# Hybrid encoder kernel: every third expert-input weight tile is split by two DMAs, with slots of its own

## The chip, the cores and the metric

The kernel runs on one core of one Trainium2 chip. The metric is device time in microseconds (us), from one launch that computes both layers. The engines are named as in the profile: PE is TensorE's matmul, PEld its weight load, DVE is VectorE, ACT is ScalarE, POOL is GpSimd, SP is SyncE, which here only issues DMAs.

## The reference

Two layers over 256 tokens of width 1024, all in float32. A layer is a mixer (RMSNorm, one input projection, five groups of heads, a norm per group, one output projection, residual) and then a PEER expert layer. The expert layer is where the changed tiles are:

```python
q = (xn @ wq).reshape(b, s, PEER_HEADS, 2, PEER_HALF)
sc = jnp.einsum('bshjc,hjkc->bshjk', q, subkeys)
top_s, top_i = lax.top_k(sc, PEER_TOPK)
...
idx = i1 * PEER_N_KEYS + i2
g = jax.nn.softmax(best, axis=-1)
...
act = jax.nn.gelu(jnp.einsum('ckd,cd->ck', u_tab[ic], xc), approximate=False)
return jnp.einsum('ck,ckd->cd', (gc * act).astype(v_tab.dtype), v_tab[ic])
```

Each token takes 16 experts of 16384 in each of 8 heads. The kernel computes the products of every expert with every token and multiplies by a gate that is zero for experts that a token did not choose.

## The kernel before, in words

**Tiles.** All weights pass through one stream of 612 tiles of 128 x 1024 float32 (512 KB), 306 a layer: 4 of w_kv, 20 of w_in, 10 of w_out, 16 of wq, 128 of the expert table u_t, 128 of v_t. PE multiplies in the format fp32r. To keep float32's accuracy, each tile is split into a high part (w_hi, the tile cast to fp32r) and a low part (w_lo, the tile less its high part), and each product is three matmuls: w_hi with the high and with the low part of the other operand, and w_lo with its high part.

**Stream.** Class Stream (L56) does this. SP loads a tile into a raw slot (w_raw, L70; pool raw, three slots). ACT casts it into a high slot (w_hi, L82), DVE subtracts into a low slot (w_lo, L84; pool hl, three slots of each); in a few mixer tiles POOL subtracts. A raw slot is free when the subtraction has read it; high and low slots are free when PE's last matmul of that tile is done. `next` hands out the parts of the next tile, and `fill` runs the loads up to 4 and the splits up to 3 tiles ahead of the tile handed out. The splits are given high priority.

**Stages of a layer.** The mixer (L308) works on w_kv, w_in and w_out. Then the expert layer (`peer_phase`): 16 tiles of wq give queries; the U stage takes the tiles of u_t in pairs (`u_pair`, 24 matmuls of 256 columns a tile, L240 to L242) and puts the gelu of the products into a large tile H; the V stage takes the tiles of v_t (`v_units`, 12 matmuls of 512 columns a tile, L269 to L273). For V, H is split in its turn, two tiles at a time, into a_hi (ACT, L954) and a_lo (DVE, L956). Beside wq and the first U tiles the routing runs on DVE and POOL: scores, searches for the largest (L810 to L814), sums of candidates on POOL (L825, L828). Beside later U tiles the gates are made: DVE writes one-hot tiles (L901, L906), and PE multiplies them (L916, 16 matmuls for a pair of U tiles).

**What sets the order.** The program is written in the order above; a scheduler that goes by a model of the engines' times then fixes a queue for each engine, in which instructions run in order. A tile of a pool waits until the last reader of the slot's former tile is done.

Of the kernel before, what the change touches and what calls it, by code (L numbers as in the profile page):

```python
# [10 lines left out]
F32 = mybir.dt.float32  # L11
F32R = mybir.dt.float32r
# [4 lines left out]
ALU = mybir.AluOpType  # L17
# [3 lines left out]
P = 128  # L21
T = 256
D = 1024
NC = D // P
NK = 128
# [3 lines left out]
SPLIT_AHEAD = 300  # L29
LIMIT = 3  # L30
AFTER = 3
MEM_CHUNK = 2
# [23 lines left out]
class Stream:  # L56


    def __init__(self, tc, raw_pool, hl_pool, sources, ahead, split_ahead):
        self.tc, self.nc, self.raw_pool, self.hl_pool, self.sources = tc, tc.nc, raw_pool, hl_pool, sources  # L60
        self.ahead, self.split_ahead = ahead, split_ahead
        self.raw, self.parts = {}, {}
        self.n_raw = self.n_parts = self.pos = 0
        self.limit = len(sources)
        self.after = ()

    def fill(self, upto=None):
        while self.n_raw < min(len(self.sources), self.pos + self.ahead, upto or len(self.sources)):
            t = self.raw_pool.tile([P, D], F32, name="w_raw")
            self.last_load = self.nc.sync.dma_start(t, self.sources[self.n_raw][0])  # L70
            self.raw[self.n_raw] = t
            self.n_raw += 1
        while self.n_parts < min(self.n_raw, self.pos + self.split_ahead, self.limit):
            r = self.raw.pop(self.n_parts)
            with ExitStack() as ctx:
                ctx.enter_context(self.tc.high_priority(SPLIT_AHEAD))
                for ins in self.after:
                    ctx.enter_context(self.tc.issue_after(ins.ins))
                self.after = ()
                hi = self.hl_pool.tile([P, D], F32R, name="w_hi")  # L80
                lo = self.hl_pool.tile([P, D], F32R, name="w_lo")
                self.nc.scalar.copy(hi, r)  # L82
                on_pool = self.sources[self.n_parts][1]
                (self.nc.gpsimd if on_pool else self.nc.vector).tensor_sub(lo, r, hi.bitcast(F32))  # L84
            self.parts[self.n_parts] = (hi, lo)
            self.n_parts += 1

# [49 lines left out]
def build(tc, x, mem, w_in, w_kv, w_out, wq, u_t, v_t, subk, pool_w, conv_pw, vec, dist, inv_count, ind, out, depth=2,  # L137
          dbg=None):
    nc = tc.nc
    V, A, G = nc.vector, nc.scalar, nc.gpsimd  # L140

    sources = []

    def queue(aps, pool_every=0):
        sources.extend((ap, pool_every > 0 and n % pool_every == pool_every - 1) for n, ap in enumerate(aps))

    for l in range(depth):
# [3 lines left out]
        queue([wq[l, b] for b in range(16)])  # L151
        queue([u_t[l, i] for i in range(NK)])
        queue([v_t[l, i] for i in range(NK)])

    with (
        tc.tile_pool(name="const", bufs=1) as cp,
        tc.tile_pool(name="raw", bufs=3) as raw_pool,
        tc.tile_pool(name="hl", bufs=3) as hl_pool,
        tc.tile_pool(name="xn", bufs=1) as xp,
# [13 lines left out]

        ind_t = cp.tile([P, 3, P], F32, name="ind_t")
        ones_m, ind64, ind32 = ind_t[:, 0, :], ind_t[:, 1, :], ind_t[:, 2, :]
        iota_b = cp.tile([P, 16, 16], BF16, name="iota_b")
# [131 lines left out]
        def mixer_phase(l, mp, pa):  # L308
# [9 lines left out]
            def mt(shape, name, bufs=1, dt=F32, tag=None):  # L318
                return mp.tile(shape, dt, name=name, tag=tag or name, bufs=bufs)

            if not l:
                mem_t = mt([P, NC, T], "mem_t", tag="df_kz")
                mem_load(mem_t, vecs, FIRST)
                stream.fill()
                nc.sync.dma_start(ind_t, ind)
                nc.sync.dma_start(xt, x.rearrange("(a p) d -> p a d", p=P))
# [759 lines left out]
```

## Time and profile before

| what | us |
|---|---|
| median of 3 runs | 2009.11 (2007.75 to 2009.66) |
| the profiled execution, its own time | 2009.29 |
| its span, first to last instruction | 2007.1 |
| PE busy | 1965.0 (98%) |
| DVE busy | 1440.1 (72%) |
| ACT busy | 1005.3 (50%) |
| POOL busy | 153.0 (8%) |
| DMA: 331.5 MB, share of 16 engines on SP's queue | 48% |

Busy shares are averages over stages that differ. Mean durations of matmuls overlap, since PE is pipelined; what a matmul costs is read from the distance between starts, or from a stretch's length divided by its matmuls. PE's granted clock is 0.995 of full speed over the span.

### The profile page before, as it was taken

The numbers are of one execution on the slowest core, as the hardware profiler recorded it, in microseconds if no ns is written. First come the engines' busy times: TensorE is split into PE (matmuls) and PEld (weight loads), VectorE is DVE, ScalarE is ACT, GpSimd is POOL, SyncE is SP. The second block draws the span as 40 slices with busy tenths as digits, with TensorE's granted clock in tenths as the row PEclk, the third lists the DMA queues.
The fourth block names the chain that finished last, engine by engine and source line by source line (L and its number), as shares of the span: only waits on it lengthen the run. The fifth ranks groups of instructions, "written<-read, shape, count | busy, mean of one in ns | idle before, by whom it ended". The sixth has DMA issues, their size and how long they took to land.

```text
span 2007.1 us, 33754 instructions
## 1 busy us (share of the span) xinstructions
PE 1965.0 (98%) x13122; PEld 1808.6 (90%) x13122; DVE 1440.1 (72%) x2791; ACT 1005.3 (50%) x1482; POOL 153.0 (8%) x197
## 2 busy tenths in 40 slices
PE   8889999999999999999999999999999999999999
PEld 7878999999999888888898789999999998888887
DVE  6975899788985655555578668997889755555555
ACT  6664455444444544444476654644443444444443
POOL 3720000000000000000037200000000000000000
PEclk9999999999999999999999999999999999999999
DMA  6324455433445555555543244454434455555554
GB/s 215 116 74 163 170 175 171 162 137 137 147 148 183 200 195 189 190 193 193 189 165 116 84 168 168 169 179 148 148 134 140 149 187 189 190 195 192 189 191 155
DMA packets 92769, 331.50 MB, mean 165 GB/s; under 512 B 10817, under 2 KB 11713, under 8 KB 92353
## 3 DMA queue, kind: packets, MB, share of 16 engines
q1 hardware_dynamic: 92608, 329.34, 48.0%
q8 instruction: 103, 1.69, 0.3%
q14 instruction: 58, 0.47, 0.1%
HBM read 328.25 MB, written 1.05 MB: 164 GB/s over the span
## 4 chain that ended last, share of the span: by engine, by line
PE 89%; DVE 4%; POOL 2%; ACT 2%; issue 1%; DMA 0%; SPq 0%; DVEq 0%; POOLq 0%; ACTq 0%
PE ps_mm L240 15%; PE ps_mm L241 15%; PE ps_mm L242 15%; PE acc_v L270 12%; PE acc_v L273 12%; PE acc_v L269 12%; PE ps_g L916 6%; POOL cv_ac L438 1%; DVE w_lo L84 1%; PE ps_sc L804 1%; ACT w_hi L82 1%; PE acc_o L269 1%; PE acc_o L273 1%; PE acc_o L270 1%; PE ps_t L227 0%
## 5 line engine op out<-in xcount | busy, mean ns | idle before, releaser
L84 DVE TENSOR_TENSOR w_lo<-w_raw,w_hi 128x1024 fp32r<-128x1024 f32 x602 | 743.4, 1235 | 417.9 <-ACT w_hi L82 417.6
L82 ACT CAST w_hi<-w_raw 128x1024 fp32r<-128x1024 f32 x612 | 641.5, 1049 | 741.7 <-PE ps_mm L241 488.0
L240 PE MATMUL ps_mm<-xh,w_hi 128*128 128x256 f32 x2624 | 752.4, 288 | 0.3 <-ACT xh L230 0.3
L242 PE MATMUL ps_mm<-xh,w_lo 128*128 128x256 f32 x2624 | 745.7, 285 | 2.1 <-DVE w_lo L84 2.0
L241 PE MATMUL ps_mm<-xl,w_hi 128*128 128x256 f32 x2624 | 746.6, 285 | 0.0
L242 PEld LDWEIGHTS ps_mm<-xh,w_lo 128*128 128x128 f32 x2624 | 504.8, 192 | 3.6 <-DVE w_lo L84 2.9
L241 PEld LDWEIGHTS ps_mm<-xl,w_hi 128*128 128x128 f32 x2624 | 505.5, 193 | 0.9 <-DVE xl L231 0.5
L240 PEld LDWEIGHTS ps_mm<-xh,w_hi 128*128 128x128 f32 x2624 | 504.2, 193 | 1.4 <-ACT xh L230 0.9
L270 PE MATMUL acc_v<-w_lo,a_hi 128*128 128x512 f32 x1016 | 316.3, 392 | 0.0
L273 PE MATMUL acc_v<-w_hi,a_lo 128*128 128x512 f32 x1016 | 315.2, 392 | 0.0
L269 PE MATMUL acc_v<-w_hi,a_hi 128*128 128x512 f32 x1016 | 273.9, 391 | 0.0
L273 PEld LDWEIGHTS acc_v<-w_hi,a_lo 128*128 128x128 f32 x1016 | 190.8, 188 | 42.4
L269 PEld LDWEIGHTS acc_v<-w_hi,a_hi 128*128 128x128 f32 x1016 | 190.8, 188 | 41.9
L270 PEld LDWEIGHTS acc_v<-w_lo,a_hi 128*128 128x128 f32 x1016 | 190.9, 188 | 40.7
L954 ACT CAST a_hi<-H 128x512 fp32r<-128x512 f32 x128 | 79.4, 622 | 153.7 <-PE acc_v L270 150.1
L956 DVE TENSOR_TENSOR a_lo<-H,a_hi 128x512 fp32r<-128x512 f32 x128 | 88.6, 693 | 77.9 <-ACT a_hi L954 77.9
L906 DVE TENSOR_SCALAR ag<-iota_f,i1T,gT 128x128 f32<-128x128 f32 x512 | 142.4, 340 | 0.0
L916 PE MATMUL ps_g<-ag,a 128*128 128x128 f32 x1024 | 125.1, 275 | 0.0
L916 PEld LDWEIGHTS ps_g<-ag,a 128*128 128x128 f32 x1024 | 120.2, 192 | 0.0
L901 DVE TENSOR_TENSOR a<-iota_f,i2T 128x1024 f32<-128x1024 f32 x64 | 77.7, 1217 | 1.7 <-PE ps_g L916 1.7
L921 DVE TENSOR_TENSOR H<-ps_g,H 128x184 f32<-128x184 f32 (+31 forms) x128 | 58.8, 463 | 1.2 <-ACT H L920 1.2
L200 POOL MEMSET mm_kz<- 128x1024 f32 x2 | 1.9, 952 | 707.4 <-PE acc_v L260 707.4
(245 smaller groups left out, 1420.6 us busy)
## 6 DMA issues: line engine op xcount, KB each, us to landing
w_raw<-u_t SPq DMA_DIRECT2D x256, 512.0 KB, 3.3
w_raw<-v_t SPq DMA_DIRECT2D x256, 512.0 KB, 4.3
w_raw<-w_in SPq DMA_DIRECT2D x40, 512.0 KB, 3.3
w_raw<-wq SPq DMA_DIRECT2D x32, 512.0 KB, 3.3
w_raw<-w_out SPq DMA_DIRECT2D x20, 512.0 KB, 3.3
w_raw<-w_kv SPq DMA_DIRECT2D x8, 512.0 KB, 4.3
H<-subk SPq DMA_DIRECT2D x2, 1024.0 KB, 4.7
mem_t<-mem SPq DMA_DIRECT2D x4, 256.0 KB, 6.3
```

The costliest lines, as they stand in the source:

```text
L82: self.nc.scalar.copy(hi, r)
L84: (self.nc.gpsimd if on_pool else self.nc.vector).tensor_sub(lo, r, hi.bitcast(F32))
L240: nc.tensor.matmul(ps, wh, xh[:, c, :], start=(c == 0), stop=False)
L241: nc.tensor.matmul(ps, wh, xl[:, c, :], start=False, stop=False)
L242: nc.tensor.matmul(ps, wl, xh[:, c, :], start=False, stop=(c == NC - 1))
L269: nc.tensor.matmul(accs[tt][hf], ah[:, s], hi[:, n], start=start, stop=False)
L270: nc.tensor.matmul(accs[tt][hf], ah[:, s], lo[:, n], start=False, stop=False)
L273: nc.tensor.matmul(accs[tt][hf], al[:, s], hi[:, n], start=False, stop=False)
L906: V.tensor_scalar(ag[:, t, :], iota_f, i1T[:, k:k + 1], gT[:, k:k + 1], op0=ALU.is_equal, op1=ALU.mult)
L916: nc.tensor.matmul(ps[:, t, :], a2[:, 4 * q + t, :], ag[:, 4 * q + t, :], start=True, stop=True)
L954: A.copy(ah, src)
L956: V.tensor_sub(al, src, ah.bitcast(F32))
```

## The change

The list of sources now says how each tile is split: on DVE (an empty mark), on POOL, or by DMAs ("dma"). The last are the u_t tiles 9, 12, 15 and so on to 117, 37 in each layer: those whose number in the stream is 2 modulo 3, within tiles 8 to 119 of u_t. Such a tile is not loaded raw. POOL issues a DMA that casts it from DRAM into the high slot. ACT writes minus the high part into the low slot. POOL then issues a second DMA of the same float32 tile that adds to the low slot. The cast is put out up to 6 tiles ahead, the second step up to 5.

High and low slots come in two classes: tiles with a number of 2 modulo 3 (all of them, in every stage) have two slots of their own; the other two thirds share two. So there are four high and four low slots where there were three. Raw slots go from three to two, for all stages. A small table of indicators (ind_t) moves from a pool that lasts for the whole kernel into the mixer's pool, and is loaded in each layer.

```diff
+DMA_U = (8, 120)
+CAST_AHEAD = 6
+LOW_AHEAD = 5
...
+    def slots(self, n):
+        tag, self.last_slot = ("d", n) if n % 3 == 2 else ("", self.last_slot)
+        return [self.hl_pool.tile([P, D], F32R, name=name, tag=name + tag) for name in ("w_hi", "w_lo")]
...
+            src, how = self.sources[self.n_raw]
+            if how != "dma":
+                t = self.raw_pool.tile([P, D], F32, name="w_raw")
+                self.last_load = self.nc.sync.dma_start(t, src)
+                self.raw[self.n_raw] = t
             self.n_raw += 1
...
+            if self.sources[n][1] == "dma":
+                continue
...
-                hi = self.hl_pool.tile([P, D], F32R, name="w_hi")
-                lo = self.hl_pool.tile([P, D], F32R, name="w_lo")
+                hi, lo = self.slots(n)
                 self.nc.scalar.copy(hi, r)
...
+        while self.n_cast < min(end, self.pos + CAST_AHEAD):
+            src, how = self.sources[self.n_cast]
+            if how == "dma":
+                if self.last_slot < self.n_cast - 3:
+                    break
+                hi, lo = self.slots(self.n_cast)
+                self.nc.gpsimd.dma_start(hi, src)
+                self.parts[self.n_cast] = (hi, lo)
+            self.n_cast += 1
+        while self.n_low < min(self.n_cast, self.pos + LOW_AHEAD):
+            src, how = self.sources[self.n_low]
+            if how == "dma":
+                hi, lo = self.parts[self.n_low]
+                with self.tc.high_priority(SPLIT_AHEAD):
+                    self.nc.scalar.mul(lo, hi.bitcast(F32), -1.0)
+                    self.nc.gpsimd.dma_start(lo, src, accum_op=ALU.add)
+            self.n_low += 1
...
-        queue([u_t[l, i] for i in range(NK)])
+        for i in range(NK):
+            sources.append((u_t[l, i], "dma" if len(sources) % 3 == 2 and DMA_U[0] <= i < DMA_U[1] else ""))
...
-        tc.tile_pool(name="raw", bufs=3) as raw_pool,
-        tc.tile_pool(name="hl", bufs=3) as hl_pool,
+        tc.tile_pool(name="raw", bufs=2) as raw_pool,
+        tc.tile_pool(name="hl", bufs=2) as hl_pool,
...
+            ind_t = mt([P, 3, P], "ind_t")
+            ones_m, ind64, ind32 = ind_t[:, 0, :], ind_t[:, 1, :], ind_t[:, 2, :]
...
-                nc.sync.dma_start(ind_t, ind)
+            nc.sync.dma_start(ind_t, ind)
```

What the change does to the queues is shown at two places. In the rows below, the words in brackets are what an instruction waits for: DMAHW is a DMA that SP issued, DMASW one that POOL issued, the others are engines.

ACT's queue in the middle of the first V stage, before (the number behind a name tells one tile of it from the next):

```order
L954 CAST a_hi_8459<-H_1895 128x512 [waits PE_49]
L82 CAST w_hi_8425<-w_raw_8401 128x1024 [waits DMAHW4_49,DVE_49,PE_49]
L82 CAST w_hi_8443<-w_raw_8423 128x1024 [waits DMAHW5_49,DVE_49,PE_49]
L954 CAST a_hi_8499<-H_1895 128x512 [waits PE_49]
L82 CAST w_hi_8465<-w_raw_8441 128x1024 [waits DMAHW6_49,DVE_49,PE_49]
L82 CAST w_hi_8483<-w_raw_8463 128x1024 [waits DMAHW7_49,DVE_49,PE_49]
```

The same place in the changed kernel:

```order
L987 CAST a_hi_8422<-H_1895 128x512 [waits DVE_49,PE_49]
L97 CAST w_hi_8388<-w_raw_8364 128x1024 [waits DMAHW7_49,DVE_49,PE_49]
L97 CAST w_hi_8406<-w_raw_8386 128x1024 [waits DMAHW0_49,DVE_49,PE_49]
L987 CAST a_hi_8462<-H_1895 128x512 [waits PE_49]
L97 CAST w_hi_8428<-w_raw_8404 128x1024 [waits DMAHW1_49]
L97 CAST w_hi_8446<-w_raw_8426 128x1024 [waits DMAHW2_49,DVE_49,PE_49]
```

The sequence is the same; every third cast, that of a tile with slots of its own, has lost its wait for PE and waits for its load alone. SP's queue in V is a row of loads in both kernels, each waiting for a subtraction on DVE: of the tile whose raw slot it takes.

POOL's queue from the routing of the first half of the tokens (sums of candidates in H) onwards, before:

```order
L825 TENSOR_TENSOR H<-H 128x8x2 x3
L828 TENSOR_TENSOR H<-H 128x8x8 [waits DVE_49]
L825 TENSOR_TENSOR H<-H 128x8x16 [waits DVE_49]
L825 TENSOR_TENSOR H<-H 128x8x8 [waits DVE_49]
L825 TENSOR_TENSOR H<-H 128x8x5
```

The same place in the changed kernel:

```order
L858 TENSOR_TENSOR H<-H 128x8x2 x3
L861 TENSOR_TENSOR H<-H 128x8x8 [waits DVE_49]
L107 DMA w_hi<-u_t 128x1024 [waits PE_49,Activation_49]
L858 TENSOR_TENSOR H<-H 128x8x16 [waits DVE_49]
L116 DMA w_lo<-u_t 128x1024 [waits PE_49,Activation_49]
L107 DMA w_hi<-u_t 128x1024 [waits DVE_49,PE_49]
L116 DMA w_lo<-u_t 128x1024 [waits PE_49,Activation_49]
L107 DMA w_hi<-u_t 128x1024 [waits DMASW0_49,PE_49]
```

The DMAs of the split tiles now stand among the sums, in the same queue. Five tiles' DMAs (u_t 9 to 21) stand before the sums of the second half of the tokens, and the cast DMA of tile 24 stands behind most of them.

## Rows read from the trace of the kernel before

**Rows 1.** The page: busy time and share, and the chain that ended last, by engine.
```profile
PE 1965.0 (98%) x13122; PEld 1808.6 (90%) x13122; DVE 1440.1 (72%) x2791; ACT 1005.3 (50%) x1482; POOL 153.0 (8%) x197
...
PE 89%; DVE 4%; POOL 2%; ACT 2%; issue 1%; DMA 0%; SPq 0%; DVEq 0%; POOLq 0%; ACTq 0%
```

**Rows 2.** Stretches: mixer, three of U, V. Length, busy by engine, clock, DMA share, GB/s.
```profile
20.00:156.00 136.00, 122.55 (x854) 111.78 (x854) 103.50 (x180) 89.32 (x175) 63.87 (x55) 1.00 0.34 115
...
228.00:312.00 84.00, 84.00 (x705) 84.00 (x705) 80.06 (x329) 46.76 (x52) 6.22 (x18) 1.00 0.48 167
...
380.00:600.00 220.00, 220.00 (x1869) 220.00 (x1869) 189.51 (x391) 94.21 (x177) 0.00 (x0) 1.00 0.41 142
600.00:645.00 45.00, 45.00 (x377) 45.00 (x376) 24.42 (x24) 20.19 (x24) 0.00 (x0) 1.00 0.56 188
645.00:1010.00 365.00, 365.00 (x1650) 301.89 (x1649) 211.51 (x209) 177.19 (x207) 1.23 (x2) 1.00 0.57 192
```

**Rows 3.** Chain in order of time, U with gates: start, length, what (two successive pairs).
```profile
388.37 1.78 PE ps_g L916 x16
395.91 1.78 PE ps_g L916 x16
```

**Rows 4.** Timeline, V: start, length, engine, instruction, idle before and its releaser; SP merged.
```profile
700.61 0.62 ACT L954 CAST a_hi<-H 128x512 fp32r<-128x512 f32 x1 [1.23 <-PE acc_v L270]
...
701.14 1.05 ACT L82 CAST w_hi<-w_raw 128x1024 fp32r<-128x1024 f32 x1
...
702.22 1.23 DVE L84 TENSOR_TENSOR w_lo<-w_raw,w_hi 128x1024 fp32r<-128x1024 f32 x1 [0.26 <-ACT w_hi L82]
...
703.82 1.05 ACT L82 CAST w_hi<-w_raw 128x1024 fp32r<-128x1024 f32 x1 [1.63 <-PE acc_v L273]
...
704.90 1.23 DVE L84 TENSOR_TENSOR w_lo<-w_raw,w_hi 128x1024 fp32r<-128x1024 f32 x1 [1.46 <-ACT w_hi L82]
...
706.10 0.62 ACT L954 CAST a_hi<-H 128x512 fp32r<-128x512 f32 x1 [1.23 <-PE acc_v L270]
...
689.68 38.78 SPq L70 DMA_DIRECT2D w_raw<-v_t  x15
```

**Rows 5.** Raw loads, issue to landing: in 690 to 816, 380 to 590, 860 to 1000.
```profile
DMA to landing us min/median/max: 3.0/3.2/4.3
...
DMA to landing us min/median/max: 3.0/3.3/4.5
...
DMA to landing us min/median/max: 4.1/4.3/4.5
```

**Rows 6.** The start: one piece of the chain (DMA), then ACT, DVE and SP timelines.
```profile
2.12 6.03 DMA w_raw<-w_kv
...
8.17 1.04 ACT L82 CAST w_hi<-w_raw 128x1024 fp32r<-128x1024 f32 x1 [0.71 <-DMA w_raw<-w_kv]
...
6.68 1.23 DVE L84 TENSOR_TENSOR w_lo<-w_raw,w_hi 128x1024 fp32r<-128x1024 f32 x1 [2.55 <-ACT w_hi L82]
...
9.25 1.23 DVE L84 TENSOR_TENSOR w_lo<-w_raw,w_hi 128x1024 fp32r<-128x1024 f32 x1 [0.55 <-ACT w_hi L82]
...
4.46 0.46 SPq L70 DMA_DIRECT2D w_raw<-w_kv  x1
...
10.50 0.33 SPq L70 DMA_DIRECT2D w_raw<-w_in  x1
```

**Rows 7.** POOL's timeline: the sums for the second half of the tokens.
```profile
297.75 2.49 POOL L825 TENSOR_TENSOR H<-H 128x64 f32<-128x64 f32 x7 [57.52 <-DVE H L810]
...
300.93 0.42 POOL L825 TENSOR_TENSOR H<-H 128x128 f32<-128x128 f32 x1 [0.42 <-DVE H L813]
```

**Rows 8.** Raw loads issued in the first 9 us: issue to landing.
```profile
DMA to landing us min/median/max: 4.4/6.5/8.0
```

**Rows 9.** Line L906, the gates' one-hots: duration in ns (min/median/max), first and last start.
```profile
L906 DVE TENSOR_SCALAR ag<-iota_f,i1T,gT x512: 328/341/349, 314.3 to 1577.3; 128x128 f32<-128x128 f32 x171
```

More of the change, by code (lines that the diff above doesn't have):

```diff
@@ L62, in __init__ @@
         self.raw, self.parts = {}, {}
-        self.n_raw = self.n_parts = self.pos = 0
+        self.n_raw = self.n_parts = self.n_cast = self.n_low = self.pos = 0
+        self.last_slot = -1
         self.limit = len(sources)
         self.after = ()
+    def slots(self, n):
+        tag, self.last_slot = ("d", n) if n % 3 == 2 else ("", self.last_slot)
+        return [self.hl_pool.tile([P, D], F32R, name=name, tag=name + tag) for name in ("w_hi", "w_lo")]
     def fill(self, upto=None):
[L68 to L71, printed above, removed]
+        end = len(self.sources)
+        while self.n_raw < min(end, self.pos + self.ahead, upto or end):
+            src, how = self.sources[self.n_raw]
[3 more added lines that the diff above has]
+                self.raw[self.n_raw] = t
             self.n_raw += 1
         while self.n_parts < min(self.n_raw, self.pos + self.split_ahead, self.limit):
-            r = self.raw.pop(self.n_parts)
+            n = self.n_parts
+            self.n_parts += 1
+            if self.sources[n][1] == "dma":
+                continue
+            r = self.raw.pop(n)
             with ExitStack() as ctx:
@@ L79, in fill @@
                 self.after = ()
-                hi = self.hl_pool.tile([P, D], F32R, name="w_hi")
-                lo = self.hl_pool.tile([P, D], F32R, name="w_lo")
+                hi, lo = self.slots(n)
                 self.nc.scalar.copy(hi, r)
-                on_pool = self.sources[self.n_parts][1]
+                on_pool = self.sources[n][1] == "pool"
                 (self.nc.gpsimd if on_pool else self.nc.vector).tensor_sub(lo, r, hi.bitcast(F32))
-            self.parts[self.n_parts] = (hi, lo)
-            self.n_parts += 1
+            self.parts[n] = (hi, lo)
+        while self.n_cast < min(end, self.pos + CAST_AHEAD):
[15 more added lines that the diff above has]
+            self.n_low += 1
     def release(self, after):
@@ L144, in queue @@
     def queue(aps, pool_every=0):
-        sources.extend((ap, pool_every > 0 and n % pool_every == pool_every - 1) for n, ap in enumerate(aps))
+        sources.extend((ap, "pool" if pool_every > 0 and n % pool_every == pool_every - 1 else "") for n, ap in enumerate(aps))
     for l in range(depth):
@@ L172, in load_vecs @@
             return t
-        ind_t = cp.tile([P, 3, P], F32, name="ind_t")
-        ones_m, ind64, ind32 = ind_t[:, 0, :], ind_t[:, 1, :], ind_t[:, 2, :]
         iota_b = cp.tile([P, 16, 16], BF16, name="iota_b")
@@ L324, in mixer_phase @@
                 stream.fill()
-                nc.sync.dma_start(ind_t, ind)
+            nc.sync.dma_start(ind_t, ind)
+            if not l:
                 nc.sync.dma_start(xt, x.rearrange("(a p) d -> p a d", p=P))
```

## The prediction

> **What bounds the kernel now.** I read the page's busy shares and its chain first: TensorE (PE) is busy 98% of the span and is 89% of the chain that ended last [rows 1]. Then the busy time by stretch [rows 2]: from 228 to 1010 us, which is the whole U stage and V stage of a layer, PE is busy for the full length of every stretch. Its idle time, 42.1 us of 2007.1, lies in the mixers (13.5 us of the 136 in layer 0) and around the start and the ends. So in U and V the time is a number of matmuls times their step, and the reader should see that nothing VectorE (DVE) or ScalarE (ACT) gives up there can shorten it: DVE is 95% busy in 228 to 312, 54% in 600 to 645, and PE is full in both. What a U tile takes: with gate matmuls 7.54 us a pair, 3.77 us a tile [rows 3]; without them 45.0 us for 377 matmuls, 0.119 us each, 24 to a tile, 2.87 us. A V tile takes half of the time from one a_hi to the next, 5.49 / 2 = 2.745 us [rows 4]. The question is therefore only whether the split parts still arrive in time, and where the new supply line is slower than 2.745, 2.87 or 3.77 us a tile.
>
> **The supply line of one tile before.** A load by SP takes 3.2 to 3.3 us to land (medians of two stretches), 4.3 at its worst there; in 860 to 1000 us every load takes 4.1 to 4.5 [rows 5]. The cast takes 1.05, the subtraction 1.23 [rows 4]. The gaps are small: a load that landed at 2.12 + 6.03 = 8.15 was cast at 8.17 (0.02), the cast ended at 9.21 and the subtraction began at 9.25 (0.04), it ended at 10.48 and the next load went out at 10.50 (0.02) [rows 6]: 0.08 in all. A raw slot is thus held for load + 1.05 + 1.23 + 0.08 = load + 2.36 us. With three raw slots that allows a tile each (3.3 + 2.36) / 3 = 1.89 us, or 2.22 at 4.3, both far under 2.745. So in V the cast waits for the high slot, which PE sets free, and not for its load: casts start 2.68 us apart right after a PE event [rows 4].
>
> **Part 1: two raw slots for three.** This touches every tile that is still loaded raw. In V all 256 tiles are. Two slots allow a tile each (load + 2.36) / 2. Load 3.2: 2.78 us. 3.3: 2.83. 4.3: 3.33. All three are above the 2.745 that PE needs; they are equal at a load of 5.49 - 2.36 = 3.13 us. I take 3.35 for the load: the two quiet medians average 3.25 and I put one load in ten at the late 4.3 (a choice between none and all). That gives 5.71 / 2 = 2.855 us a tile, 0.11 more than PE needs, 14.1 us over the 128 tiles of one V stage. There is a cushion: a cast starts two PE tiles (5.49 us) before its tile's turn and cast and subtraction take 2.3, so 3.2 us are eaten before PE waits. 14.1 - 3.2 = 10.9 us a layer, **21.8 us** for both. Ends: load 3.2 throughout, 0.035 x 128 = 4.5, less 3.2, 1.3 a layer, 2.6 in all; three in ten late (3.25 + 0.3 = 3.55), 0.21 x 128 = 26.9, less 3.2, 47 in all. That the late landing does not stay for good I take from the loop itself: at 4.3 the next load goes out 0.5 us later, so it finds its predecessor further ahead; before, PE's pace held the spacing at 38.45 / 14 = 2.746 us [rows 4] whatever the landing did.
>
> In wq and in U before tile 8 and after 119 all tiles are raw too, at 2.87 us or more a tile: 2.855 fits, cost 0. In the middle of U two of three tiles use the two slots, 8.6 us for each slot's use: 5.7 fits. In the mixer a tile takes some 4 us (34 in 136) and 5.7 / 2 fits; the load of a tile goes out one subtraction later than before, and PE's idle time there hangs on other chains. I take 0, with 3 us either way for the new order.
>
> At the start the third w_kv load, out at 4.46 us, must wait for the first subtraction, which ends at 6.68 + 1.23 = 7.91 [rows 6]: 3.4 us later. PE has two tiles of work before it, at the start's pace; I take 0, at most 3.
>
> **Part 2: slots of their own.** A tile whose number is 2 modulo 3 has two slots, used every sixth tile; the others share two, used every third. So the others wait for tile n - 3 as with three slots, and in V the casts of the third class lose their PE wait. Nothing is lost; it also gains nothing, since the load is now what is late.
>
> **Part 3: 74 tiles (37 a layer) through two DMAs.** Each takes a subtraction of 1.23 from DVE, 91 us of DVE time in all, on an engine that PE did not wait for: worth 0. The cast of 1.05 on ACT becomes a multiplication of the same shape: 0. It adds 74 x 512 KB, 39 MB or 12%, where DMA is about half busy (0.41 to 0.57 [rows 2]): hidden. The new waits: POOL issues the cast DMA when tile n - 6 is done, ACT's multiplication waits for its landing, POOL's accumulating DMA waits for that. Five tiles lie between, 14.4 us without gates and 18.9 with. A DMA from POOL, a cast or an add in a DMA stand in no row. From below: like SP's load, 3.3 + 1.05 + 3.3 = 7.7 us. From above: the slowest w_raw load of the trace, 8.0 us in the crowded start [rows 8], twice: 17.1. I take the lower end plus some 2 us for each DMA, about 12, since DMA is half idle in U and was crowded there: hidden, 0. A page has a price: the Trainium skill, "DMA: Bandwidth & Descriptors", in "Anatomy of one DMA", gives for POOL-issued transfers 2.0 us plus the bytes at 436 GB/s, 3.2 us here; by it the chain is 7.5 us and also hidden, and no row here shows it.
>
> Behind the waiting multiplication on ACT stand casts of the next tiles (ahead of PE by 3.2 us) and gelu; a landing later than about 4 us eats into that. On POOL the DMAs stand in line with the routing's adds, which wait for DVE: the second group ran at 297.75 to 301.4 [rows 7], and the cast DMA of U tile 24 is now queued behind it, with PE at that tile around 300. But in the order of the two kernels 71 subtractions precede the last search of that group before, 62 after: nine fewer on DVE, 9 x 1.23 = 11 us, so the group ends at about 290 and leaves some 10 us. Cost 0; 5 us a layer if the group does not move.
>
> **The sum.** Span 2007.1 + 21.8 = 2028.9; the profiled run took 2009.29 us beside its span of 2007.1, and the median of the three runs is 2009.11, so they are the same run for this purpose. 2009.3 + 21.8 = 2031.1. Forecast **2031 us**; its own range 2012 to 2057.
>
> **Rivals.**
> - *Not slower:* the load takes no more than 3.13 us (3.18 with the cushion: 0.025 x 128 = 3.2) once nothing else is in flight, and V stays on PE's pace. Decides at 3.18. For: the shortest are 3.0, the median 3.2. Against: two loads still overlap. Time 2009 to 2012.
> - *Faster:* the mixers, where PE idles 13.5 us, come out in a better order and V is not hurt. It needs over 4 us of some 27 in both layers. Time 2003.
> - *The late landing stays:* all V loads at 4.3, as in 860 to 1000. 0.585 x 128 = 75, less 3.2, 72 a layer, 143 in all: 2153; in one layer only, about 2092. Against it: the wider spacing, above.
> - *The two DMAs are not hidden:* the chain exceeds 14.4 us. A class slot turns once in six tiles, one of them its own, so a tile then takes chain / 5. The one-hots begin at 314.3 [rows 9]: (314.3 - 228) / 2.87 = 30 tiles without gates, 21 of them behind the first split by DMAs. At 17.1: 3.42, 0.55 over 2.87, 11.5 a layer, 23 on top: 2054. At 10 us a DMA (21 in all): 1.33 x 21 + 0.43 x 76 gated tiles (286 us at 3.77) = 61 a layer: 2153. What speaks for it: a sum in SBUF must be read as well as written, and DVE's one-hots, 512 of 341 ns [rows 9], could hold POOL up. The Trainium skill, "SBUF — State Buffer", in "Who interferes with whom", says that tensor_scalar on DVE can take a port pair that POOL needs and block it for the instruction; by it each DMA's issue waits up to a 0.34 us instruction, in bursts of four 1.4, and the gated limit falls from 18.9 to about 16; whether these take that mode no row shows.
>
> **Chances and range.** Forecast 0.56; not slower 0.15; faster 0.05; late landing stays 0.10; DMAs not hidden 0.14. A measurement of this kernel can tell 0.2% (4 us) from no change. Faster 0.05, same 0.15, slower 0.80. The range 2008 to 2085 leaves out faster (0.05), nearly all of the stuck landing (0.09) and the far part of the last rival (0.05).
>
> **What would show it.** In V the casts should wait for DMA w_raw<-v_t in place of PE, SP should issue some 2.85 us apart, PE should show waits for w_lo, and each V stage should be about 11 us longer, U unchanged. Wrong if V's tiles stay at 2.745 us; if U holds PE waits for w_hi or w_lo; if a mixer moves by over 3 us.

## The result and the profile after

The changed kernel takes **2087.1 us** (median of 4 runs, 2083.1 to 2094.6) where the kernel before takes 2009.4: 1.0394 times as long, 95% interval 1.0382 to 1.0407, some 78 us more. The forecast was 2031 us, slower by 21.8, with a range of 2008 to 2085. The direction was right; the size was far off, and the time lies just above the range.

The page of after, engines and the chain that ended last, by engine and by line (compare [rows 1]):

```profile
PE 2011.8 (96%) x13122; PEld 1807.8 (86%) x13122; DVE 1353.1 (65%) x2717; ACT 1003.4 (48%) x1482; POOL 265.8 (13%) x345
...
PE 39%; DMA 24%; DVE 15%; ACT 9%; issue 9%; POOL 2%; SPq 0%; ACTq 0%; DVEq 0%; POOLq 0%
DMA w_raw<-v_t 19%; DVE w_lo L99 10%; PE ps_mm L272 9%; PE ps_mm L270 9%; PE ps_mm L271 9%; ACT w_hi L97 8%; PE ps_g L949 5%; DVE cv_ac L467 1%; DMA w_raw<-u_t 1%; DMA w_raw<-w_in 1%; DMA w_hi<-u_t 1%; PE acc_v L300 1%; POOL H L858 1%; PE acc_v L303 1%; PE acc_v L299 1%
```

PE was 89% of the chain and is 39%. DMA went from 0 to 24%, and 19% of the span is the loads of v_t alone: V no longer runs at PE's pace. Stretches of after that answer to [rows 2], with the columns named there: mixer, U beside the routing, U with gates, U's last tiles, V:

```profile
20.00:156.00 136.00, 119.36 (x812) 109.62 (x813) 101.47 (x179) 87.99 (x173) 63.07 (x55) 0.95 0.32 112
242.00:326.00 84.00, 82.64 (x687) 81.82 (x687) 78.83 (x342) 45.11 (x50) 19.83 (x33) 1.00 0.73 208
400.00:615.00 215.00, 215.00 (x1827) 215.00 (x1827) 169.29 (x377) 91.46 (x173) 27.34 (x38) 1.00 0.69 189
615.00:660.00 45.00, 45.00 (x377) 45.00 (x376) 20.14 (x22) 20.12 (x24) 3.74 (x5) 1.00 0.70 212
680.00:1045.00 365.00, 357.21 (x1505) 276.34 (x1504) 193.45 (x196) 166.03 (x196) 0.00 (x0) 1.00 0.53 181
```

The reader sees three places, not one. In 365 us of V there are 1505 matmuls where there were 1650. Beside the routing PE is no longer full (82.64 of 84). The mixer's mean clock fell from 1.00 to 0.95. With gates and in U's last tiles PE is as full as it was, and the pairs keep the pace of [rows 3]: from the 24th to the 48th of the 64 pairs after's delay against before stays within 1 us.

To divide the whole, I cut each layer at the first matmul of the scores, and at the first and the last matmul of V. In a view of one tile's instructions (durations in ns, then first and last start) those cuts of after's first layer are at 203.1, 677.6 and 1050.0, the starts that these rows give first, first and last:

```profile
L837 PE MATMUL ps_sc<-H x64: 269/275/276, 203.1 to 284.9; 128*128 128x128 f32 x64
...
L299 PE MATMUL acc_v<-w_hi,a_hi x508: 387/392/505, 677.6 to 1045.3; 128*128 128x512 f32 x170
...
L290 PE MATMUL acc_v<-w_hi,a_lo x4: 387/396/398, 1048.6 to 1050.0; 128*128 128x512 f32 x4
```

Stage lengths in us, all of profiled runs. "Mixer" runs up to the first score (with wq), "U" from there to V. After's profiled run, 2094.6 us, was the longest of its four, 7.5 above the median, so the parts below add up to 85 and not to 78. A ratio is to the runs of before that were taken beside it, and need not be the quotient of the medians shown.

| kernel | mixer 0 / 1 | U 0 / 1 | V 0 / 1 | median us | ratio to before (95%) |
|---|---|---|---|---|---|
| before | 189.1 / 174.7 | 467.8 / 467.8 | 351.3 / 351.3 | 2009.4 | |
| after | 203.1 / 190.7 | 474.6 / 475.6 | 372.3 / 370.9 | 2087.1 | 1.0394 (1.0382 to 1.0407) |
| e1_raw2 | 192.7 / 181.9 | 479.8 / 476.6 | 372.4 / 376.4 | 2088.0 | 1.0398 (1.0381 to 1.0415) |
| e2_nodma | 198.7 / 191.2 | 477.1 / 478.6 | 373.3 / 370.7 | 2097.5 | 1.0438 (1.0421 to 1.0456) |
| e3_raw3mv | 206.5 / 187.8 | 476.7 / 473.1 | 353.6 / 351.3 | 2051.6 | 1.0202 (1.0185 to 1.0219) |
| e4_ind | 189.9 / 174.6 | 467.8 / 467.8 | 351.3 / 351.3 | 2008.9 | 0.9996 (0.9987 to 1.0006) |
| e6_noclass | 192.6 / 176.0 | 479.3 / 474.4 | 351.3 / 351.3 | 2028.2 | 1.0087 (1.0070 to 1.0103) |
| e7_class | 205.3 / 187.1 | 467.8 / 467.8 | 351.3 / 351.3 | 2038.0 | 1.0143 (1.0126 to 1.0160) |
| e8_raw2u | 192.0 / 174.1 | 481.7 / 476.1 | 351.3 / 351.3 | 2035.1 | 1.0130 (1.0113 to 1.0147) |
| e9_poolneg | 194.5 / 174.2 | 501.9 / 495.4 | 351.3 / 351.3 | 2075.7 | 1.0320 (1.0274 to 1.0365) |
| e10_freeneg | 191.9 / 175.0 | 472.4 / 471.0 | 351.3 / 351.3 | 2023.1 | 1.0068 (1.0051 to 1.0084) |
| e11_raw3u | 191.9 / 174.3 | 475.1 / 477.4 | 351.3 / 351.3 | 2029.4 | 1.0093 (1.0072 to 1.0115) |
| e12_class_raw4 | 196.2 / 184.4 | 467.8 / 467.8 | 351.3 / 351.3 | 2026.3 | 1.0085 (1.0068 to 1.0102) |
| e13_raw4 | 187.2 / 174.2 | 467.8 / 467.8 | 351.3 / 351.3 | 2007.4 | 0.9991 (0.9982 to 1.0001) |
| e14_noprio | 204.3 / 187.9 | 467.8 / 467.8 | 351.3 / 351.3 | 2034.2 | 1.0120 (1.0100 to 1.0140) |
| e15_classout | 189.9 / 174.8 | 467.8 / 467.8 | 351.3 / 351.3 | 2010.4 | 1.0007 (0.9997 to 1.0016) |
| e16_noadd | 193.7 / 175.1 | 470.3 / 468.1 | 351.3 / 351.3 | 2014.4 | 1.0023 (1.0014 to 1.0033) |

After against before: V +21.0 and +19.6, the mixers +14.0 and +16.0, U +6.8 and +7.8.

**V, read in the trace.** Timelines of after in the first V stage, ACT, DVE and SP (idle time and its releaser in brackets), for [rows 4]:

```profile
861.92 1.05 ACT L97 CAST w_hi<-w_raw 128x1024 fp32r<-128x1024 f32 x1 [1.11 <-DMA w_raw<-v_t]
864.86 1.05 ACT L97 CAST w_hi<-w_raw 128x1024 fp32r<-128x1024 f32 x1 [1.89 <-DMA w_raw<-v_t]
...
863.01 1.23 DVE L99 TENSOR_TENSOR w_lo<-w_raw,w_hi 128x1024 fp32r<-128x1024 f32 x1 [0.85 <-ACT w_hi L97]
...
841.90 47.81 SPq L82 DMA_DIRECT2D w_raw<-v_t  x18
```

In [rows 4] the casts waited for PE; here they wait for their loads, as forecast (225 of V's 256, over both layers). Landings from the page's list of DMA issues (KB each, median us to landing):

```profile
w_raw<-v_t SPq DMA_DIRECT2D x256, 512.0 KB, 3.3
w_raw<-u_t SPq DMA_DIRECT2D x182, 512.0 KB, 4.2
w_hi<-u_t POOLq DMA_DIRECT2D x74, 512.0 KB, 5.4
w_lo<-u_t POOLq DMA_DIRECT2D x74, 512.0 KB, 5.3
```

The median of the v_t loads fell to 3.3 (before, the page has 4.3). But the mean over all 256, from each issue to its last landing, is 3.44, with 15% over 4.0 and the longest 5.1. A row of tiles through two slots goes by the mean. From its load's issue to the end of its subtraction a tile held its raw slot for 5.84 us in the mean, and the slot's next load went out 0.03 later: 5.87 / 2 = 2.93 us a tile, the mean distance of SP's issues in both V stages. PE kept before's pace for some 12 tiles of the first V stage and some 20 of the second, and then fell behind by about 0.18 us a tile.

**U, read in the trace.** Beside the routing, timelines of ACT, then PE, then POOL:

```profile
298.84 1.06 ACT L115 ACTIVATE w_lo<-w_hi 128x1024 fp32r<-128x1024 f32 x1 [4.04 <-DMA w_hi<-u_t]
300.16 1.05 ACT L97 CAST w_hi<-w_raw 128x1024 fp32r<-128x1024 f32 x1 [0.27 <-DMA w_raw<-u_t]
...
308.96 1.06 ACT L115 ACTIVATE w_lo<-w_hi 128x1024 fp32r<-128x1024 f32 x1 [5.02 <-DMA w_hi<-u_t]
309.93 1.03 ACT L97 CAST w_hi<-w_raw 128x1024 fp32r<-128x1024 f32 x1
...
312.27 0.39 PE L272 MATMUL ps_mm<-xh,w_lo 128*128 128x256 f32 x1 [0.30 <-DVE w_lo L99]
...
316.64 0.39 PE L272 MATMUL ps_mm<-xh,w_lo 128*128 128x256 f32 x1 [1.04 <-DMA w_lo<-u_t]
...
304.49 1.44 POOL L107 DMA_DIRECT2D w_hi<-u_t  x1
```

ACT stands 4 to 5 us at the multiplication until the cast DMA has landed; the cast of the next, ordinary tile starts directly behind it. PE then waits for that tile's subtraction (312.27), or for the adding DMA itself (316.64). The tile at 308.96 and 316.64 is u_t 24: its cast DMA left POOL at 304.49, amid the routing's sums. Over the whole of after (us in total, times, longest):

```profile
ACT w_hi L97 <- DMA w_raw<-v_t: 382.8, 225, 3.8
ACT w_lo L115 <- DMA w_hi<-u_t: 167.2, 59, 5.9
PEld acc_v L300 <- DVE w_lo L99: 41.7, 139, 0.5
PE ps_mm L272 <- DVE w_lo L99: 9.4, 14, 2.6
PE ps_mm L272 <- DMA w_lo<-u_t: 2.8, 5, 1.0
```

### The profile page after: what moved, and what is told of

The parts are those of the page before. It is cut to its first block, busy times and chain, and to the rows that moved or that the text cites. A ratio compares the mean times of both kernels' runs of the same rounds, so it can differ in the third digit from the quotient of the medians.

```text
span 2092.8 us, 33700 instructions
## 1 busy us (share of the span) xinstructions
PE 2011.8 (96%) x13122; PEld 1807.8 (86%) x13122; DVE 1353.1 (65%) x2717; ACT 1003.4 (48%) x1482; POOL 265.8 (13%) x345
## 3 DMA queue, kind: packets, MB, share of 16 engines
q0 software_dynamic: 21312, 77.60, 16.4%
HBM read 367.25 MB, written 1.05 MB: 176 GB/s over the span
## 4 chain that ended last, share of the span: by engine, by line
PE 39%; DMA 24%; DVE 15%; ACT 9%; issue 9%; POOL 2%; SPq 0%; ACTq 0%; DVEq 0%; POOLq 0%
DMA w_raw<-v_t 19%; DVE w_lo L99 10%; PE ps_mm L272 9%; PE ps_mm L270 9%; PE ps_mm L271 9%; ACT w_hi L97 8%; PE ps_g L949 5%; DVE cv_ac L467 1%; DMA w_raw<-u_t 1%; DMA w_raw<-w_in 1%; DMA w_hi<-u_t 1%; PE acc_v L300 1%; POOL H L858 1%; PE acc_v L303 1%; PE acc_v L299 1%
## 5 line engine op out<-in xcount | busy, mean ns | idle before, releaser
L99 DVE TENSOR_TENSOR w_lo<-w_raw,w_hi 128x1024 fp32r<-128x1024 f32 x528 | 650.1, 1232 | 641.9 <-ACT w_hi L97 634.3
L97 ACT CAST w_hi<-w_raw 128x1024 fp32r<-128x1024 f32 x538 | 563.1, 1047 | 762.8 <-DMA w_raw<-v_t 382.8
L300 PE MATMUL acc_v<-w_lo,a_hi 128*128 128x512 f32 x1016 | 328.2, 403 | 1.4
L299 PE MATMUL acc_v<-w_hi,a_hi 128*128 128x512 f32 x1016 | 278.2, 394 | 13.1 <-ACT w_hi L97 13.1
L300 PEld LDWEIGHTS acc_v<-w_lo,a_hi 128*128 128x128 f32 x1016 | 179.8, 188 | 73.2 <-DVE w_lo L99 41.7
L115 ACT ACTIVATE w_lo<-w_hi 128x1024 fp32r<-128x1024 f32 x74 | 78.4, 1060 | 167.5 <-DMA w_hi<-u_t 167.2
L116 POOL DMA_DIRECT2D w_lo<-u_t x74 | 65.2, 881 | 488.3 <-ACT w_lo L115 369.5
```

The source lines that it names most:

```text
L299: nc.tensor.matmul(accs[tt][hf], ah[:, s], hi[:, n], start=start, stop=False)
L300: nc.tensor.matmul(accs[tt][hf], ah[:, s], lo[:, n], start=False, stop=False)
```

## The experiments

Three questions: which part of the change costs V, which the mixers, which U. The theory at the start was that the missing raw slot is behind both V and the mixers, and the POOL DMAs behind U. Only its first clause and part of its last held.

### Raw slots

**e1_raw2**, one size of the kernel before:

```diff
-        tc.tile_pool(name="raw", bufs=3) as raw_pool,
+        tc.tile_pool(name="raw", bufs=2) as raw_pool,
```

> The kernel before with two raw slots for three and nothing else changed. Theory A (the missing raw slot is behind the V stages and the mixers): each V stage 371 us for 351, the first mixer 203 for 189 and the second 190 for 175, U as before at 468; about 2009 + 40 + 30 = 2079 us. Rival B (the mixers lose by the new order of instructions, that is by the indicator table and the slot classes, not by the raw slots): V stages 371, mixers as before; 2049 us. By my prediction's sum: 2031 us.

2088.0 us, as much as the whole change. V is 372.4 and 376.4, where after has 372.3 and 370.9: the raw slot alone costs V that much. (e1's second V stage had slower loads, 3.49 us in the mean for the first's 3.42.) The mixers lose only 3.6 and 7.2, not 14 and 16, and U loses 12.0 and 8.8, which neither theory had. The nearly equal totals of e1 and after are not the same loss.

**e3_raw3mv** goes the other way: after with the third raw slot given back where there is room.

```diff
-                t = self.raw_pool.tile([P, D], F32, name="w_raw")
+                k = self.n_raw % 306
+                if self.n_raw % 3 == 2 and self.extra and (4 <= k < 34 or k >= 184):
+                    t = self.extra.tile([P, D], F32, name="w_raw", tag="w_raw_x")
+                else:
+                    t = self.raw_pool.tile([P, D], F32, name="w_raw")
```

> The changed kernel with a third raw slot in the mixers (in the mixer's pool, for tiles of w_in and w_out) and in V from its seventh tile (in the room of the routing's tables); U keeps two raw slots and its DMAs. Theory A: V stages back to 351 to 353, mixers back to 189 and 175 within 3 us each, U stays 7 to 8 us longer than before; 2009 + 15 to 20 = 2024 to 2029 us. Rival B: V back, mixers not; 2054 us. Rival E (V's loads are late for another reason than the slots, such as what the POOL DMAs leave behind): V stays at 371, 2064 us or more.

V is back at 353.6 and 351.3, and its casts wait for PE again:

```profile
ACT w_hi L102 <- PE acc_v L308: 192.8, 117, 4.4
...
ACT w_hi L102 <- DMA w_raw<-v_t: 23.4, 18, 2.3
```

The mixers stay at 206.5 and 187.8 with three raw slots. So what they lose in after is not the raw slot, and theory A falls there.

**e8_raw2u** takes the slot away in U (with w_kv, wq and V's first six tiles), by the same lines in the kernel before.

> The kernel before with two raw slots for w_kv, wq, U and the first six tiles of V, and three in the rest of the mixers and of V. Theory J (in U two slots bind beside the routing, where the subtraction waits in DVE's queue, and the raw slot is held that much longer): U 476 to 480 for 468 in both layers, mixers and V as before within 3 us; 2009 + 16 to 26 = 2025 to 2035 us. Rival K (two slots suffice in U, and what the run with two raw slots lost there came from outside U): U 468 to 470, 2009 to 2015 us.

U is 481.7 and 476.1, V as before, the mixers 192.0 and 174.1: theory J. Of layer 0, 2.9 us are in the mixer, where w_kv has two slots at the start. The delay against before grows up to the 24th of the 64 pairs of U tiles and then stays the same within 0.1 us to the 48th: two slots bind beside the routing only. There a raw slot was held for 6.7 us (mean of 35 tiles in e1, 60 to 180 us behind the first score): 3.7 to the cast, 1.05, 0.76 waiting in DVE's queue, 1.22. Half of that is 3.35 us a tile, over PE's 2.87, and the casts stood 3.31 apart (3.04 in the same stretch of before).

### Slot classes

**e4_ind**, the indicator table alone:

```diff
-        ind_t = cp.tile([P, 3, P], F32, name="ind_t")
...
+            ind_t = mt([P, 3, P], "ind_t")
```

> The kernel before with the indicator table in the mixer's pool and loaded in each layer; three raw slots and all else as before. Theory A: 2009 us, within 4. Rival B (the moved table and the order that follows from it is what the mixers lose by): up to 14 and 16 us longer mixers, 2039 us.

No change. **e7_class** puts the classes alone into the mixers of before, with three raw slots:

```diff
+                n = self.n_parts
+                pool, tag = self.hl_pool, ""
+                if n % 3 == 2:
+                    pool, tag = (self.extra, "d1") if 4 <= n % 306 < 34 and n // 3 % 2 else (self.hl_pool, "d0")
```

> The kernel before with the slot classes in the mixers alone (tiles of w_in and w_out with a number of 2 modulo 3 have two high and two low slots, the second from the mixer's pool), three raw slots everywhere, no DMA splits. Theory F: mixers 200 to 206 and 185 to 191 us, all else as before; 2009 + 11 to 16 + 11 to 16 = 2031 to 2041 us. Rival G: 2009 us within 4.

Mixers 205.3 and 187.1: +16.2 and +12.4 from the classes alone. **e6_noclass** undoes them outside U, in e3's kernel:

```diff
-        tag, self.last_slot = ("d", n) if n % 3 == 2 else ("", self.last_slot)
+        tag = "d1" if 50 <= n % 306 < 178 and n // 3 % 2 else "d0"
```

> As the run with the third raw slot back in the mixers and in V (e3_raw3mv, 2051.6 us), but tiles with a number of 2 modulo 3 have two high and two low slots only in U; in the mixers, wq and V they have one, so that there every cast again waits for the tile three before. Theory F (the slot classes are what the mixers lose by: every third cast and subtraction runs ahead of other work of ACT, DVE and POOL): mixers back to 189 and 175 within 4 us each, U 473 to 477, V 351 to 354; 2018 to 2026 us. Rival G (the mixers lose by something else that the changed kernel brings): mixers stay at 206 and 188, 2050 us.

Mixers 192.6 and 176.0, so theory F holds both ways. U at 479.3 in the first layer is 2 over what was expected. Slots that free the casts from PE cost the mixers 12 to 16 us a layer. How? The input part of the mixer, before (first row) and in e7 (second), each up to its first w_out matmul:

```profile
15.00:117.00 102.00, 94.10 (x722) 89.92 (x722) 79.83 (x124) 69.85 (x138) 56.31 (x50) 1.00 0.40 139
```
```profile
15.00:132.00 117.00, 100.86 (x712) 95.77 (x711) 84.14 (x121) 68.42 (x127) 61.43 (x52) 0.91 0.37 129
```

PE's idle time grows from 7.9 to 16.1 us and the clock falls to 0.91. One of the places, in ACT's timeline of e7:

```profile
29.94 1.04 ACT L85 CAST w_hi<-w_raw 128x1024 fp32r<-128x1024 f32 x1 [2.27 <-DMA w_raw<-w_in]
30.89 0.47 ACT L233 ACTIVATE xh<-ps_t,vecs 128x256 fp32r<-128x256 f32 x1
```

A cast that needs no slot of PE's any more is placed early in ACT's queue, its load is not there, and the first xh of the norm, which PE needs, stands behind it: at 30.89, where before it ran at 27.13:

```profile
27.13 0.47 ACT L230 ACTIVATE xh<-ps_t,vecs 128x256 fp32r<-128x256 f32 x1 [0.70 <-PE ps_t L227]
```

The load that this cast waits for, landed at 29.92, is the stream's ninth, number 8, which is 2 modulo 3; number 7, landed at 25.24, is cast after it, at 41.45 at the earliest.

**e12_class_raw4** gives e7 a fourth raw slot in the mixers and loads one tile further ahead; **e13_raw4** does that to before.

```diff
+            if 6 <= k < 34 and k % 4 == 0:
+                t = self.extra.tile([P, D], F32, name="w_raw", tag="w_raw_x")
...
-        while self.n_raw < min(len(self.sources), self.pos + self.ahead, upto or len(self.sources)):
+        while self.n_raw < min(len(self.sources), self.pos + self.ahead + (6 <= self.n_raw % 306 < 34), upto or len(self.sources)):
```

> As e7_class (slot classes in the mixers of the kernel before, 2038.0 us; mixers 205.3 and 187.1), with a fourth raw slot in the mixers and their loads issued one tile further ahead. Theory M (the classes cost what they do because ACT stands at casts whose loads have not landed): mixers back to within 4 us of 189 and 175, 2007 to 2017 us. Rival N (the casts that run ahead displace the mixer's own work in the queues of ACT and DVE, whenever their loads land): mixers stay at 200 to 206 and 184 to 190, 2030 to 2040 us.

> The kernel before with a fourth raw slot in the mixers and their loads issued one tile further ahead, no classes: the control for e12_class_raw4, and a version that could beat both. If the mixers' idle time hangs on loads, up to 5 us less in each, 2000 to 2005 us; if it hangs on the mixer's own chains, as the waits of before say, 2009 us within 4.

e13 cannot be told from before: the best of all these kernels is not shown to beat it. e12's mixers are 196.2 and 184.4: earlier loads give back 9 of 16 us in layer 0, but only 3 of 12 in layer 1. ACT's waits at casts for loads of w_in and w_out go the same way: 2.0 and 0 us in the two mixers before (from 15 us on), 13.5 and 4.9 in e7, 6.6 and 5.2 in e12. So e12 did not take all of these waits away, and what is left does not decide between the theories. Nor does such a wait cost PE its whole length: e1 has some 12 us of them in each mixer. **e14_noprio** takes the priority from those splits:

```diff
+                if not (self.n_parts % 3 == 2 and 4 <= self.n_parts % 306 < 34):
+                    ctx.enter_context(self.tc.high_priority(SPLIT_AHEAD))
```

> As e7_class (2038.0 us; mixers 205.3 and 187.1), but in the mixers the split of a tile that has slots of its own is not put ahead of other work by its priority. Theory N (splits that run ahead take the place of the mixer's own work in the queues of ACT and DVE): mixers back to within 5 us of 189 and 175, 2009 to 2019 us. Rival M (only the loads that are not there at such a cast count): mixers within 3 us of 205 and 187, 2034 to 2042 us.

204.3 and 187.9: nothing comes back, so priority is not it. The same cast still stands before that xh (at 30.73, after 2.88 us of waiting), so this run does not say what an order without such casts would cost. **e15_classout** has `24 <= n % 306 < 34` in e7's line, the classes for w_out alone.

> As e7_class, but with the slot classes for the tiles of w_out alone. If the out projection's 3 to 4 us (54.0 and 55.6 for 50.9 and 51.2) come from its own tiles, they stay and the input part is as before (117 and 103 us): 2009 + 7 = 2016 us. If they are a late echo of the input part, both are as before: 2009 us within 3.

2010.4 us; the stretch of the w_out matmuls is 51.9 and 51.9 us (50.9 and 51.2 before, 54.0 and 55.6 in e7). Most of what the out projection loses in e7 is not by its own tiles: it comes with the classes in the input part. So the classes act in the input part, partly by casts that stand waiting for loads; what the rest is (7 us in layer 0 and 10 in layer 1 with the fourth slot) stays open.

### The split by DMAs in U

**e2_nodma**, after without any split by DMAs:

```diff
-DMA_U = (8, 120)
+DMA_U = (0, 0)
```

> The changed kernel with no tile split by DMAs (all 74 are loaded raw and split by ACT and DVE); two raw slots, the slot classes and the moved indicator table stay. Theory A: V and mixers as in the changed kernel, and U goes back to 468 to 470 a layer, as the POOL DMAs are what costs 7 us there; 2087 - 14 = 2073 us. Rival C (U loses by two raw slots too, not by the DMAs): U stays at 475, 2087 us. Rival D (the DMAs pay for part of their cost, since two of three tiles then share the raw slots): U is longer than 475 and the time above 2087 us.

Rival D: U is longer than after's, by 2.5 and 3.0 us (477.1 and 478.6), and the median is 10 us above after's, more than U accounts for. Given two raw slots, the DMA splits pay for themselves, since their tiles need no raw slot. But U still loses 7 to 8 us in after. Is that the raw slots that are left, or the splits themselves?

**e11_raw3u** lends U, up to tile 39, raw slots in the one-hots' idle buffers, on e6's kernel:

```diff
+                if self.extra_u and 38 <= k < 90:
+                    raw = (self.extra_u, dict(tag="ag", bufs=2)) if self.n_loads % 3 == 2 else (self.raw_pool, {})
```

> As e6_noclass (2028.2 us), but from wq to U tile 39 every third raw load goes to slots of the one-hots' buffers, which are idle there: at least three raw slots in the stretch where U fell behind, with the DMA splits as they are. Theory H: U stays at 479 and 474 within 3 us, 2025 to 2031 us. Rival L: U 468 to 472 and 468 to 470, 2014 to 2019 us.

2029.4 us and U 475.1 and 477.4, where e6 has 479.3 and 474.4: 4 us shorter in one layer, 3 longer in the other, and no gain in all. This run alone does not clear the raw slots, since the one-hots wait for the lent ones and begin 13 and 16 us later behind the first score than before's. (A delay of 6.5 and 8.3 us is there at the 16th pair, ahead of them.) What clears them is e16 below, with the same two raw slots.

**e9_poolneg** moves the negation to POOL. It was built on e6's kernel, not on e3's as its expectation says, so it stands against 2028.2 us.

```diff
-                    self.nc.scalar.mul(lo, hi.bitcast(F32), -1.0)
+                    self.nc.gpsimd.tensor_scalar(lo, hi.bitcast(F32), -1.0, None, op0=ALU.mult)
```

> As e3_raw3mv (2051.6 us), but minus the high part is written by POOL, not by ACT. Theory H (what U loses to the split by DMAs is ACT standing at the multiplication until the cast DMA has landed, with the next tiles' casts behind it): U 468 to 470 in both layers, and so 2051.6 - 14 + 3 = 2038 to 2042 us. Rival I (the chain of cast DMA, negation and adding DMA itself is late for PE, and POOL's queue with it): U stays at 473 to 477 or grows, 2050 us or more.

2075.7 us, U 22 us longer than e6 in each layer. POOL's negation, and what PE then waits for:

```profile
L123 POOL TENSOR_SCALAR w_lo<-w_hi 128x1024 fp32r<-128x1024 f32 x74 | 218.7, 2955 | 394.9 <-DMA w_hi<-u_t 202.6 <-issue 84.8 <-PE ps_mm L280 53.9
```
```profile
PE ps_mm L280 <- DMA w_lo<-u_t: 39.4, 23, 5.1
```

The negation takes 2.96 us for ACT's 1.06, in the queue that issues the DMAs too, and PE waits 39.4 us for the adding DMA where e6 has 3.0. If that is the chain, longer by 1.9 us, and not POOL's fuller queue, then it is hidden in after by a small margin only. The run does not decide on theory H, which it confounds with a longer chain.

**e10_freeneg** takes the wait itself away, and **e16_noadd** the adding DMA on top:

```diff
-                    self.nc.scalar.mul(lo, hi.bitcast(F32), -1.0)
-                    self.nc.gpsimd.dma_start(lo, src, accum_op=ALU.add)
+                    self.nc.scalar.mul(lo, self.free, -1.0)
```

(`free` is the residual stream's tile; e10 keeps the line that is taken out second. Both leave out the right low part of these tiles.)

> As e6_noclass (2028.2 us; U 479.3 and 474.4), but ACT's multiplication for a DMA-split tile reads a tile that is always there (the residual stream) and not the high part, so that it never stands waiting for the cast DMA; this leaves the right low part out, and shortens the chain of the two DMAs as well. Theory H (what U loses is ACT standing at that multiplication with the next tiles' casts behind it): U falls to 468 to 472 and 468 to 470, 2014 to 2019 us. Rival L (the two raw slots, for the tiles that are still loaded raw beside the routing): U stays at 479 and 474 within 2 us, 2026 to 2030 us.

> As e10_freeneg (2023.1 us; U 472.4 and 471.0), with the adding DMA left out as well, so that half of the DMA traffic of the split is gone and PE waits for no DMA into a low slot; the low part of these tiles is left out. If the rest of U's loss (4.6 and 3.2 us) is the adding DMA's late landing or the traffic, U is 468 to 469 in the second layer and within 3 us of 468 in the first, 2016 to 2019 us. If the rest is the raw slots or the cast DMA, U stays at 471 to 473, 2021 to 2025 us.

Without the wait U falls from 479.3 and 474.4 to 472.4 and 471.0, without the adding DMA to 470.3 and 468.1. The second layer is then within 0.3 us of before's 467.8; of the 2.5 us that are left in the first, 1.8 are there at the third pair, ahead of the first tile that is split by DMAs. (After itself has no delay there.) So U's loss in this kernel is the split's own two costs: ACT standing at the multiplication, 6.9 and 3.4 us, and the adding DMA, 2.1 and 2.9. (e10 starts that DMA earlier too, so its share is not free of the chain's length.) The same 120 us beside the routing, from 60 us behind the first score, in before, e8, after and e16:

```profile
249.00:369.00 120.00, 120.00 (x1007) 120.00 (x1006) 110.13 (x342) 66.21 (x81) 3.17 (x9) 1.00 0.50 173
```
```profile
252.00:372.00 120.00, 112.61 (x918) 109.99 (x916) 106.55 (x343) 61.03 (x74) 3.13 (x9) 1.00 0.45 154
```
```profile
263.00:383.00 120.00, 116.10 (x951) 113.85 (x950) 90.34 (x313) 61.79 (x74) 23.21 (x34) 1.00 0.76 216
```
```profile
253.00:373.00 120.00, 120.00 (x1002) 119.55 (x1001) 98.09 (x344) 66.78 (x80) 13.99 (x22) 1.00 0.53 176
```

PE is full before and in e16, loses 7.4 us to two raw slots without DMA splits, 3.9 with them. The DMA share is 0.76 with the adding DMA, 0.53 without.

## Why the prediction was wrong in size

- **The bound and part 1 in V: right mechanism, mis-sized term.** A slot's hold over two, the cushion, no PE wait in the casts, PE waiting for w_lo: all there. The term was 10.9 us a layer and measured 21.0 and 19.6. What came out too small is the hold: 5.71 in the sum, 5.87 measured. Of that, 0.09 is the load, 3.44 in the mean where 3.35 was taken from two medians of [rows 5] and a guess of late ones; the rest is gaps, above all 0.08 from a landing to its cast, where [rows 6] has 0.02. With 2.93 us a tile the text's own sum gives 0.185 over PE's 2.745, 23.7 us over 128 tiles, less the cushion of 3.2: 20.5. The term is a small difference of two large times, so 0.16 us in a hold of 5.87 doubled it. The guess of one load in ten at the late landing was near the 15% measured, in part by luck: before, half of the first V stage's loads and all of the second's took over 4.0. (The longest load in the two quiet stretches of [rows 5] is 4.5, not the 4.3 of the text.) The bounds that stood there, 2.6 to 47 for both layers, held the 40.6.
- **Part 1 in the mixers, "I take 0, with 3 us either way": near in the first, too low in the second.** Raw slots cost them 3.6 and 7.2 in e1. Of the 3.6 some 3 are at the start (2.9 in e8), where the text had "0, at most 3"; what the 7.2 are was not followed up.
- **Part 2, slots of their own, "Nothing is lost": the step that failed.** It looked at what a tile must wait for, found that nothing waits longer, and missed that a queue in which instructions run in order is made anew: freed casts are placed early, and where their load is not there they hold up the mixer's own work. The mixers lost 14.0 and 16.0 us in after, 16.2 and 12.4 by the classes alone (e7). This is 30 of the 85 us and had no term. That the classes cost this is shown; that it is by casts standing at loads is shown for a part of it only (e12).
- **Part 3, the two DMAs, 0: wrong by 7 to 8 us a layer.** The chain was put at about 12 us. Measured: 5.4 for the cast DMA, 1.06, 5.3 for the adding one, 11.8 by medians, and PE waited for it only 2.8 us. By the Trainium skill, "DMA: Bandwidth & Descriptors", "Anatomy of one DMA" (2.0 us and the bytes at 436 GB/s), the estimate for a POOL-issued DMA of 512 KB is 3.2 us; both took 2 us more here. What failed is the next paragraph: it saw that casts stand behind the waiting multiplication and that a landing later than about 4 us would hurt, and took 0 all the same, although its own 12 us hold some 5.3 for each DMA. Of the 74 cast DMAs 69 took over 4 us. ACT stood at the multiplication 59 times, 2.8 us in the mean (167.2 / 59) and up to 5.9.
- **POOL's queue, 0 if the routing's group moves 11 us: the move was right, the 0 not quite.** The group began 108.7 us behind the first score (297.75 in [rows 7]) and begins 97.7 behind it in after. Still the cast DMA of u_t 24 left only at 304.49, amid these sums; ACT stood 5.02 us for it (308.96), and that tile's adding DMA is the one that PE waits for at 316.64. After's delay in the first U stage begins there: nothing at the start of the 11th pair, 0.3 us at the 12th, 2.6 at the end of the 13th, this tile's. How much of the 6.8 us is POOL's queue no run separates.
- **U with two raw slots, "8.6 for each slot's use: 5.7 fits": right where a third of the tiles bypass the raw slots (e16).** With all tiles raw (e8) it costs 13.9 and 8.3, as the hold has a wait in DVE's queue that the 5.7 left out.
- **The rivals.** "Not slower" fell: the mean load was over 3.18. The late landing did not stay, as was argued (3.44 in the mean, after 3.77 and 4.32 in before's two V stages); no run tests the argument itself. "The two DMAs are not hidden" came about in e9, not in after. Of the signs named, V's came true in kind (each stage some 20 us longer, not 11), and the two that were to speak against the forecast, U holding PE waits and a mixer moving by over 3 us, both appeared.

## What to carry to other kernels

Where a loop through few buffers sets the pace, forecast with the mean of the transfer over all of its states, not with a median, and add every gap: the loss is a small difference of two large times. A slot more is not free where a scheduler orders queues: look at what the freed instruction now stands in front of, in stages that the change does not aim at as well. Of an instruction that waits for a transfer, ask how long it stands at the head of its queue, not only whether the transfer is in time.

## What the chip showed that was not expected

- **An adding DMA costs the queues about as much as two loads.** All of POOL's DMAs took 16.4% of 16 engines over 2092.8 us in after; the cast DMAs alone 6.1% of 2014.9 us in e16. If the cast DMAs took as much in after, the 74 adding ones took 343 - 123 = 220 us, 3.0 us each on all engines, the cast DMAs 1.7; 512 KB on SP's queue before took 1.5 (48.0% of 2007.1 us for 329.34 MB, as much as 628 loads). SP's loads of u_t land at a median of 4.2 beside both, at 3.3 beside the cast DMAs alone (e16).
- **Where PE's gaps grew, the clock mostly fell too.** From 20 us to the first score, TensorE's granted clock stood at its lower level (1.2 of 2.4 GHz, 0.5 in the records) for 6.8 us in one piece before, 23.9 us in six pieces in after; PE was idle there for 16.7 and 21.9 us. In layer 1's mixer it was 13.7 and 27.3 us, with 12.3 and 21.9 idle. In e7's second mixer idle time rose as much (24.1) and the lower level stayed at 13.7 us, so the one does not follow from the other alone. As an estimate, let a us at the lower level give half a us of work: added idle time and half of the added time at the lower level make 13.8 and 16.4 us for after's mixers, which lost 14.0 and 16.0. It is rough: for e7 (idle 25.1 us and lower level 30.7 in the first mixer) it makes 20.4 and 11.8, where the loss was 16.2 and 12.4.
- **With two raw slots the loads of V landed sooner.** The mean of the v_t loads was 4.04 us before and 3.86 in e3, with three raw slots, and 3.44 to 3.46 in after, e1 and e2, with two. Why is not shown: with three slots too there is a stretch at 3.2 [rows 5].

The rows of the first point, from the pages: POOL's queue in after, POOL's queue in e16, SP's queue before (packets, MB, share of 16 engines):

```profile
q0 software_dynamic: 21312, 77.60, 16.4%
```
```profile
q0 software_dynamic: 10656, 38.80, 6.1%
```
```profile
q1 hardware_dynamic: 92608, 329.34, 48.0%
```
